# Attention with two-by-two Strassen products: splitting one product of weights and V once more

## The chip, the core and the metric

The kernel runs on one NeuronCore of a Trainium2 chip. The metric is the device time of one execution in microseconds (us). Engines are named as in the profile: PE (TensorE matmul), PEld (its weight loads), DVE (VectorE), ACT (ScalarE), POOL (GpSimd), SP (SyncE, which only issues DMAs here).

## The reference

```python
def setup_inputs():      # q, k, v: (8, 2048, 512) float32, normal
    ...
def reference(q, k, v):
    d_k = q.shape[-1]
    scores = np.matmul(q, k.transpose(0, 2, 1)) / np.sqrt(d_k)
    attn_weights = special.softmax(scores, axis=-1).astype(np.float32)
    return np.matmul(attn_weights, v)
```

## The kernel before

**Tiling.** For each of 8 batches, the 2048 queries are cut into two *spans* of 1024, and a span into two halves of 512 (4 query tiles of 128 in each half). Both matrix products are done in float16 by Strassen's scheme in Winograd's form: 7 products of half-size blocks in place of 8, with sums of blocks before and after.

**Scores (class `Group`).** A group is a pair of neighbouring key blocks (keys 2j and 2j+1, 128 keys each) against both halves of the queries; it has 7 products, each of two 128x512 matmuls (L291). The results collect in PSUM banks x, y, z. After products 1, 5 and 6 ACT copies a bank out (L301, L305, L308), after 7 and 3 DVE adds (L311, L314), after 4 and 2 ACT takes the exponential into `left[1]` and `left[0]` (the unnormalised weights of the first 512 queries), and `exp_right` takes that of 1024 columns into `right` (those of the second 512). Eight groups make a span's weights.

**Weights times V (class `Pair`).** A pair is one query tile of the first half together with one of the second; a span has 4 pairs. `left[0]`, `left[1]` are the weights of a tile of the first half for even and odd key blocks, `right` those of the second half, and V is cut by even and odd key block and by halves of its 512 columns. Each of the 7 products is a sum over 8 key-block pairs j: 8 matmuls with 256 (or 257) columns (L386). The 257th column is a column of ones, which gives the row sums of the softmax. Product 2 is `left[1]` (odd keys) times the first half of V's columns, and belongs to one output quadrant alone. After products 5 and 3 DVE takes the reciprocal of a row sum (L418, L424); ACT scales a bank by it into an output tile (L395), DVE adds the next bank, scaled, to the tile (`final`, L398), and SP stores the tile.

**Rounds and order.** The work runs in 32 rounds g, two for each span. In round g, PE does the pairs a and b of the round, and at the same time the scores of the span after (4 groups, 28 products); each engine executes strictly in the order in which the program issues to it. The order is set by lists: `QORDER` says in which order the products of two neighbouring groups alternate, `ORDER` after which score product a pair's product stands (`b7'` is product 7 of the pair b of the round before), `PLAN` when loads and DMA transposes of the next batch are issued, `KSUMS`, `VSUMS`, `SUMS0` and `sums_of` when DVE makes the sums of K, V, Q and the weights. Round 0 and the last two rounds have lists of their own (`FIRST`, `ALONE`, `LAST`); the opening, before round 0, has word lists (`SECOND`, `OPENING`).

**Buffers.** All eight PSUM banks are in use: qx (2), qy, qz for the scores, px (2), py, pz for the pairs. Output tiles come from a pool of 7, loads of K and Q from a staging pool of 3, and the weights from a pool that holds two spans.

Of the kernel before, what the change touches and what calls it, by code (L numbers as in the profile page):

```python
# [12 lines left out]
def kernel(  # L13
# [21 lines left out]
    nc = tc.nc  # L35
# [29 lines left out]
    ppool = ctx.enter_context(tc.tile_pool(name="ppool", bufs=2))  # L65
    spool = ctx.enter_context(tc.tile_pool(name="spool", bufs=2))
    opool = ctx.enter_context(tc.tile_pool(name="opool", bufs=7))
# [14 lines left out]
    ident = const.tile([P, P], F16)  # L82
    ident_dram = nc.inline_tensor(np.eye(P, dtype=np.float16), name="attn_identity")
    nc.scalar.dma_start(out=ident[:], in_=ident_dram.ap())
# [14 lines left out]
    vt4 = const.tile([P, NJ, H], F16, name="vt4")  # L99
    staged = {}  # L100
# [47 lines left out]
    def transposed(what, c, n, w, copy):  # L148
        src = staged[what, 0, c]
        tr = psum["px"].tile([P, 2, ND, P], F16, tag="px", name="tr")  # L150
        for m in range(w):
            for dc in range(ND):
                nc.tensor.transpose(  # L153
                    tr[:, m, dc, :], src[:, n + m, dc * P:(dc + 1) * P], ident[:]
                )
        copy(out=raw_of(what, 0, c)[:, n:n + w], in_=tr[:, 0:w])  # L156
        if n + w == CH:
            staged.pop((what, 0, c))
# [62 lines left out]
    def new_p(sp):  # L221
        left = [ppool.tile([P, NJ, QH], F16, tag=f"left{s}", name=f"left{s}") for s in range(2)]
        right = ppool.tile([P, NJ, 2, QH], F16, tag="right", name="right")
        pts[sp] = (left, right)
# [124 lines left out]

    class Pair:  # L350
# [3 lines left out]
        def __init__(self, g, which):  # L354
            self.g, self.which, self.done = g, which, 0

# [37 lines left out]
        def scaled(self, out_, src, r):  # L394
            nc.scalar.activation(out=out_, in_=src, func=COPY, scale=r[:])  # L395

        def final(self, out_, src, r):
            nc.vector.scalar_tensor_tensor(  # L398
                out=out_, in0=src, scalar=r[:], in1=out_, op0=MULT, op1=ADD
            )  # L400
# [14 lines left out]
        def after5(self):  # L415
            self.o2 = opool.tile([P, D], F32, tag="o")
            self.r2 = small.tile([P, 1], F32, tag="r2")
            nc.vector.reciprocal(out=self.r2[:], in_=self.z[:, H:H + 1])  # L418
            self.scaled(self.o2[:, H:D], self.z[:, 0:H], self.r2)

        def after3(self):
            self.o1 = opool.tile([P, D], F32, tag="o")
            self.r1 = small.tile([P, 1], F32, tag="r1")
            nc.vector.reciprocal(out=self.r1[:], in_=self.z[:, H:H + 1])  # L424
# [6 lines left out]
        def after6(self):  # L431
            self.scaled(self.o1[:, H:D], self.x[:, 0:H], self.r1)
# [8 lines left out]
        def after4(self):  # L441
            if not self.apart:
# [5 lines left out]
                out=self.o2[:, one], in0=self.x[:, one], scalar1=self.r2[:], scalar2=None, op0=MULT  # L448
# [7 lines left out]
    def pv(g, which):  # L456
        g -= which.endswith("'")
# [7 lines left out]
    ORDER = "a1 b7' a5 b4' a3 b1 a6 a2 a7 b5 a4 b3 b2 b6".split()  # L465
    FIRST = "a1< b1< a1> a5 b1> a3 a2 a6 a7 b5 a4 b3 b2 b6".split()
    ALONE = "b7' a1 b4' a5 b1 a3 b5 a2 a6 b3 a7 b2 b6 a4".split()
    LAST = "b7' a1 b4' a5 b1 b5 a3 a2 b3 a6 b6 a7 b7 b2 b4 a4".split()

# [3 lines left out]
    def after_slot(g):  # L473
        order = {0: FIRST, NP - 2: ALONE, NP - 1: LAST}.get(g, ORDER)
        return {2 * n + 1: x for n, x in enumerate(order)}

    PLAN = {}
    for qt_, slot_, *what_ in (  # L480
# [10 lines left out]
    ):  # L491
        PLAN.setdefault((qt_, slot_), []).append(what_)

    KSUMS = {(1, 14): 0, (2, 0): 1, (2, 16): 2, (3, 2): 3}
    background = deque()

    def prefetch(g, slot):
        b, qt = divmod(g, NQT)
        if (g, slot) == (0, 12):
            nc.gpsimd.memset(vraw[1][:, :, 1, D:D + 1], 1.0)  # L500
        for kind, what, c in PLAN.get((qt, slot), ()):
            if b + 1 < B:
                if kind == "load":
                    load_v(b + 1, c) if what == "v" else load(what, b + 1, c)
                else:
                    dma_transpose(what, b + 1, c)
        if (qt, slot) in KSUMS and b + 1 < B:
            background.extend(k_sums(KSUMS[qt, slot]))
        if background and slot in ((2, 8, 10, 14, 16, 24, 26)):
            background.popleft()()  # L510

    def sums_of(g, slot):

        if g == 0:
            return [first_sum(x) for x in SUMS0.get(slot, "").split()]
        todo = []
        if slot in (7, 9, 11, 13):
            todo.append(p_sums(g, "b")[(slot - 7) // 2])
        early = (20, 23, 25, 27) if g == NP - 2 else (17, 19, 21, 22)
        if slot in early and g + 1 < NP:  # L520
            todo.append(p_sums(g + 1, "a", 0, NJ if g % 2 == 0 else NE)[early.index(slot)])
        if slot in (4, 5) and g % 2 == 0:
            late = p_sums(g, "a", NE)
            todo.extend(late[0:2] if slot == 4 else late[2:4])
        sp = g // 2 + 2
        if slot in (23, 25, 27) and g % 2 == 1 and sp < NP // 2:
            todo.append(q_sums(sp)[(slot - 23) // 2])
        if slot == 6 and g % 2 == 0 and g < NP - 2:
            todo.append(q_sums(sp - 1)[3])
        if g % NQT == 0 and slot in VSUMS:  # L530
            for at in (i for i, s in enumerate(VSUMS) if s == slot):
                todo.append(v_sums(g // NQT, at % NCH)[at // NCH])
        return todo

    SUMS0 = {
        2: "v02",
        3: "v03",
        4: "q3",  # L540
        5: "a0",
        6: "a1",
        8: "a3",
        9: "a2",
        11: "v12 v13",
        12: "v20 v21",
        13: "v22",
        14: "b0 v23",
        15: "v30",
        16: "b1 v31",  # L550
        17: "v32",
        18: "v33",
        19: "b3",
        20: "k02",
        21: "b2",
        22: "A0",
        23: "k12 A1",
        24: "A2",
        25: "k22 A3",
        26: "k32",  # L560
    }

    def first_sum(x):
        n = int(x[1])
        if x[0] in "kv":
            return (k_sums if x[0] == "k" else lambda c: v_sums(0, c))(int(x[2]))[n]
        if x[0] == "q":
            return q_sums(1)[n]
# [205 lines left out]
```

## Time and profile before

| | |
|---|---|
| time, median of 3 runs | 800.87 us (800.75 to 801.21) |
| span of the profiled execution | 799.2 us (its page lists no other time of its own) |
| PE busy | 793.7 us, 99% |
| PEld busy | 538.1 us, 67% |
| DVE busy | 557.6 us, 70% |
| ACT busy | 572.0 us, 72% |
| POOL busy | 71.5 us, 9% |
| granted PE clock | 1.000 |

The span goes from the first instruction to the last in one execution taken by the hardware profiler. Busy time is the share in which the engine has an instruction running; matmuls are pipelined, and one's listed duration (273 ns at 256 columns) is longer than the distance to the next.

### The profile page before, as it was taken

To read this page: it belongs to the slowest core of one execution; us is meant where nothing else is said; L and a number is where in the kernel's file an instruction comes from. 1 tells how busy PE (TensorE), PEld (TensorE's weight loads), DVE (VectorE), ACT (ScalarE), POOL (GpSimd) and SP (SyncE) were. 2 spreads that over 40 slices of the span, in tenths; PEclk is the share of its full clock that TensorE was granted. 3 is DMA by queue.
4 is the path that set the end of the run, shared out by engine and by line. 5 is a ranking of instruction groups with operands and counts; after the bars stand their busy time and mean duration, and the time that the engine had idled before them with its cause. 6 is when DMAs were issued, how large, how long until landed. Compare 5 with 4: busy or idle time off the path is not lost.

```text
span 799.2 us, 14622 instructions
## 1 busy us (share of the span) xinstructions
PE 793.7 (99%) x5556; PEld 538.1 (67%) x5556; DVE 557.6 (70%) x1230; ACT 572.0 (72%) x1020; POOL 71.5 (9%) x105
## 2 busy tenths in 40 slices
PE   9999999999999999999999999999999999999998
PEld 6566666666666666666666666666666666666677
DVE  5786767857677676866768667686776857678564
ACT  4877777777777767777777777777677777776752
POOL 4011110001101010010100110001110011000000
PEclk9999999999999999999999999999999999999999
DMA  9999992899828999399994999849993598711112
GB/s 222 175 176 177 207 172 73 156 183 196 166 60 156 182 197 145 80 161 178 177 158 78 173 177 186 128 93 155 203 217 86 96 205 160 162 40 41 44 52 104
DMA packets 188870, 115.80 MB, mean 145 GB/s; under 512 B 122496, under 2 KB 171904, under 8 KB 188800
## 3 DMA queue, kind: packets, MB, share of 16 engines
q0 software_dynamic: 49648, 49.29, 42.9%
q1 hardware_dynamic: 138576, 65.16, 38.3%
q8 instruction: 43, 0.70, 0.4%
q10 hardware_dynamic: 576, 0.43, 0.2%
q14 instruction: 27, 0.22, 0.1%
HBM read 100.70 MB, written 33.55 MB: 168 GB/s over the span
## 4 chain that ended last, share of the span: by engine, by line
PE 99%; DMA 0%; DVE 0%; ACT 0%; issue 0%
PE t L386 49%; PE t L291 46%; PE t L234 1%; PE t L250 1%; PE tr L153 1%; DMA first<-in_q_dram 0%; PE t L657 0%; DVE kraw L156 0%; ACT o L395 0%; DVE stage L132 0%; DVE o L447 0%
## 5 line engine op out<-in xcount | busy, mean ns | idle before, releaser
L291 PE MATMUL t<-qraw,kraw 128*128 128x512 f16 x732 | 198.1, 379 | 0.0
L395 ACT ACTIVATE o<-t,r 128x256 f32<-128x256 f32 (+1 forms) x256 | 121.1, 473 | 100.5 <-DVE r L418 69.5
L386 PEld LDWEIGHTS <-s 128*128 128x128 f16 x1536 | 150.3, 98 | 56.5
L227 ACT ACTIVATE left<-t 128x512 f16<-128x512 f32 x256 | 154.1, 603 | 37.0 <-PE t L291 30.8
L398 DVE SCALAR_TENSOR_TENSOR o<-t,r,o 128x256 f32<-128x256 f32 x192 | 92.4, 482 | 102.1 <-PE t L386 60.9
L291 PEld LDWEIGHTS <-kraw 128*128 128x128 f16 x984 | 96.2, 98 | 64.2 <-issue 0.3
L291 PE MATMUL t<-qs,ks 128*128 128x512 f16 x492 | 136.5, 379 | 0.0
L386 PE MATMUL t<-vh,left 128*128 128x256 f16 x1024 | 133.0, 273 | 0.0
L386 PE MATMUL t<-vt,s 128*128 128x257 f16 (+1 forms) x1024 | 133.0, 273 | 0.0
L227 ACT ACTIVATE right<-cz 128x1024 f16<-128x1024 f32 x123 | 130.5, 1061 | 1.1 <-DVE cz L311 1.1
L386 PEld LDWEIGHTS <-left 128*128 128x128 f16 x1024 | 100.2, 98 | 37.6
L386 PEld LDWEIGHTS <-right 128*128 128x128 f16 x1024 | 100.2, 98 | 37.5 <-issue 0.4
L305 ACT COPY cz<-t 128x512 f32<-128x512 f32 x122 | 71.4, 585 | 72.8 <-PE t L291 72.4
L311 DVE TENSOR_TENSOR cz<-t,cz 128x512 f32<-128x512 f32 x123 | 84.5, 687 | 52.8 <-PE t L291 52.7
L314 DVE TENSOR_TENSOR cz<-t,cz 128x512 f32<-128x512 f32 x123 | 84.9, 690 | 43.0 <-PE t L291 41.6
L291 PEld LDWEIGHTS <-ks 128*128 128x128 f16 x738 | 72.1, 98 | 48.3 <-DVE ks L183 0.3
L291 PE MATMUL t<-qraw,ks 128*128 128x512 f16 x246 | 73.2, 379 | 0.0
L291 PE MATMUL t<-qs,kraw 128*128 128x512 f16 x246 | 73.2, 379 | 0.0
L301 ACT COPY t<-t 128x512 f32<-128x512 f32 x121 | 69.0, 570 | 4.0 <-PE t L291 0.8
L308 ACT COPY cz<-t 128x512 f32<-128x512 f32 x123 | 71.5, 581 | 0.0
L386 PE MATMUL t<-vh,s 128*128 128x257 f16 x512 | 66.7, 273 | 0.0
L386 PE MATMUL t<-vh,right 128*128 128x256 f16 x512 | 66.2, 273 | 0.1
(62 smaller groups left out, 574.0 us busy)
## 6 DMA issues: line engine op xcount, KB each, us to landing
out_dram<-o SPq DMA_DIRECT2D x124, 256.0 KB, 3.5
vh<-in_v_dram POOLq DMA_DIRECT2D x32, 512.0 KB, 10.5
stage<-in_k_dram POOLq DMA_DIRECT2D x29, 512.0 KB, 8.0
stage<-in_q_dram POOLq DMA_DIRECT2D x28, 512.0 KB, 7.9
right<-in_k_dram POOLq DMA_DIRECT2D x2, 512.0 KB, 13.2
out_dram<-o SPq DMA_DIRECT2D x6, 128.0 KB, 1.7
first<-in_q_dram SPq DMA_DIRECT2D x2, 256.0 KB, 3.3
cz<-in_q_dram SPq DMA_DIRECT2D x2, 256.0 KB, 4.8
```

What stands on the lines that cost most here:

```text
L153: nc.tensor.transpose(tr[:, m, dc, :], src[:, n + m, dc * P:(dc + 1) * P], ident[:])
L227: nc.scalar.activation(out=out_, in_=in_, func=EXP, scale=inv_sqrt_d)
L234: nc.tensor.matmul(st[:], kops[c][0][:, n, dc, :], qraw[0][:, half * NT:(half + 1) * NT, dc, :], start=(dc == 0), stop=(dc == ND - 1),)
L291: nc.tensor.matmul(dst[:], lhs[:, j, dc, :], rhs[:, :, dc, :], start=(n in (1, 5) and dc == 0), stop=(dc == 1), skip_group_check=True,)
L301: self.edges[0](out=self.y[:], in_=self.x[:])
L305: self.edges[1](out=self.cz[:, 1, :], in_=self.z[:])
L308: nc.scalar.copy(out=self.cz[:, 0, :], in_=self.x[:])
L311: nc.vector.tensor_add(self.cz[:, 1, :], self.x[:], self.cz[:, 1, :])
L314: nc.vector.tensor_add(self.cz[:, 0, :], self.z[:], self.cz[:, 0, :])
L386: nc.tensor.matmul(dst[:, 0:width], lhs(j), rhs(j), start=(first and j == 0), stop=(j == NJ - 1), skip_group_check=True,)
L395: nc.scalar.activation(out=out_, in_=src, func=COPY, scale=r[:])
L398: nc.vector.scalar_tensor_tensor(out=out_, in0=src, scalar=r[:], in1=out_, op0=MULT, op1=ADD)
```

## The change

In 15 of the 16 spans (all but the last), product 2 of the four pairs leaves the pairs. What it computed is one matrix product of 512 query rows x 1024 odd keys by 1024 keys x 256 columns of V for the whole span; a new class `Leaf` does it by Strassen's scheme once more. Its blocks are two query tiles by four key blocks against four key blocks by 128 columns. Each of its 7 products is 2 tiles x 4 matmuls with 128 columns, into the bank py, which the pairs of those spans no longer use.

The parts around it:

- `leaf_v_sums` are four sums of the V blocks (128x512 each) once a batch, one of them in place. `leaf_p_sums` are four sums of the weights (128x1024 each) for each span; they are written into the half of `left[0]` that the pairs have finished with.
- A pair's product 1 is now copied by ACT into an accumulator tile `acc` (`after1`), without scaling. After each leaf product, DVE adds its bank into a quarter of an accumulator. After leaf products 3 and 4 an accumulator is complete: POOL multiplies it by the reciprocals, in two instructions, and SP stores it as a half row for two tiles.
- A pair's product 6 now goes to a tile of half rows (`ohpool`) that is stored by itself; products 4 and 7 work as before.
- The leaf of a span runs in L2 and L1 in the span's second round, and in L5, L6, L3, L7, L4 in the first round of the next span.
- The weights lie in fixed tiles in place of a pool; the identity and the zeros of the opening lie in tiles of V's sums; the output pool shrinks from 7 to 3, with 3 accumulators and 2 half-row tiles beside it.
- The lists `ORDER`, `FIRST`, `ALONE`, `LAST`, `PLAN`, `KSUMS`, `VSUMS`, `SUMS0` give way to one word list for each kind of round. A "." is the next score product, "e" an `exp_right`, a, b and L are products of pairs and leaf, s, w, x, y, z, v, k, q are sums (leaf's weights, leaf's V, weights, V, K, Q), l and t are loads and transposes.

```diff
+    def leaf_p(sp):
+
+        a = pts[sp][0][1]
+        w = NT // 2 * P
+        room = pts[sp][0][0]
+        return (a[:, 0:NK, 0:w], a[:, NK:NJ, 0:w], a[:, 0:NK, w:2 * w], a[:, NK:NJ, w:2 * w],
+                room[:, NK:NJ, 0:w], room[:, NK:NJ, w:2 * w])
+
+    def leaf_p_sums(sp):
+        a11, a12, a21, a22, x, y = leaf_p(sp)
+        return {
+            1: lambda: add(x, a21, a22),
+            2: lambda: sub(y, x, a11),
+            3: lambda: sub(x, a11, a21),
+            4: lambda: sub(y, a12, y),
+        }
...
+        def product(self, n):
+            a11, a12, a21, a22, x, y = leaf_p(self.sp)
+            b11, b12, b21, b22, t1, t2, t3, t4 = leaf_v(self.sp // NSP)
+            if n in (1, 2):
+                self.t = bank("py")
+            lhs, rhs, at = {
+                1: (a11, b11, 0), 2: (a12, b21, 0), 3: (y, b22, 1), 4: (a22, t4, 0),
+                5: (x, t1, 1), 6: (y, t2, 0), 7: (x, t3, 0),
+            }[n]
+            for t in range(2):
+                to = self.t[:, (2 * at + t) * P:(2 * at + t + 1) * P]
+                for j in range(NK):
+                    nc.tensor.matmul(
+                        to, lhs[:, j, t * P:(t + 1) * P], rhs[:, j, :],
+                        start=(n in (1, 2) and t == 0 and j == 0), stop=(j == NK - 1),
+                        skip_group_check=True,
+                    )
...
+            nc.vector.tensor_add(acc, part, acc)
+            if n == 3:
+                self.store(0)
+            elif n == 4:
+                self.store(1)
+
+        def store(self, m):
+            acc = acc_of(self.sp, m)
+            for t in range(2):
+                r = r1s[:, self.sp % 2, 2 * m + t:2 * m + t + 1]
+                nc.gpsimd.tensor_scalar(
+                    out=acc[:, t, :], in0=acc[:, t, :], scalar1=r, scalar2=None, op0=MULT
+                )
...
+        def after1(self):
+            if self.leaf:
+                acc = acc_of(self.g // 2, self.i // 2)
+                nc.scalar.copy(out=acc[:, self.i % 2, :], in_=self.x[:, 0:H])
...
         def after6(self):
+            if self.leaf:
+                o = ohpool.tile([P, H], F32, tag="oh", name="oh")
+                self.scaled(o[:], self.x[:, 0:H], self.r1)
+                self.final(o[:], self.z[:, 0:H], self.r1)
...
-    ORDER = "a1 b7' a5 b4' a3 b1 a6 a2 a7 b5 a4 b3 b2 b6".split()
...
+        1: (
+            "w0 lk3 . a1 . . xb0 . b7' . lv1 e . w1 a5 . . xb1 tk1 . w3 e xb3 w2 . b4' . a3 . xb2 lk2 "
+            "a6 . . . b1 . . L2 . . k00 . tk2 e xa0 b5 xa1 a7 k20 . . . xa3 a4 s1 . q0 b3 . e . q1 q2 "
+            "k30 L1 . xa2 s2 b6 . k10 "
+        ),
...
+        0: (
+            "v01 . . L5 lq0 e v03 . a1 b7' ya0 v00 v02 s3 . ya1 L6 ya2 . . ya3 v10 a5 q3 . v11 . s4 "
+            "b4' xb0 lq1 . . e xb1 a3 v12 . L3 v21 v20 . v13 lk0 . tq0 b1 xb2 . xb3 a6 L7 . v22 . v23 "
+            "lv0 . . e v30 xa0 b5 tq1 v32 v33 . a7 xa2 . xa1 L4 . tk0 v31 . xa3 . . b3 lk1 a4 . . e . "
+            ". b6 "
+        ),
...
+        'alone': (
+            "L5 b7' . a1 s3 L6 e s4 ya0 xb0 . ya1 b4' ya3 a5 L3 b1 ya2 L7 xb1 a3 xb3 b5 L4 xb2 a6 b3 "
+            "a7 xa0 a2 b6 b2 xa2 xa1 xa3 a4 "
+        ),
+        'last': (
+            "b7' a1 a5 xb0 xb1 b4' a3 xb2 b1 xb3 b5 a2 b3 q0 a6 b6 a7 q2 b7 a4 b4 b2 q1 "
+        ),
...
```

The lists keyed 1, 2, 3, 0 stand for rounds with that remainder by 4; 0 is the round that opens a batch.

More of the change, by code (lines that the diff above doesn't have):

```diff
@@ L221, in new_p @@
     def new_p(sp):
[L222 to L224 removed]
+        pts[sp] = (lefts[sp % 2], rights[sp % 2])
     def exp(out_, in_):
@@ L350, with leaf @@
+    leaves = {}
+    def leaf(sp, n):
+        if not leaf_span(sp) or sp < 0:
+            return
+        if sp not in leaves:
+            leaves[sp] = Leaf(sp)
+        leaves[sp].product(n)
     class Pair:
@@ L456, in pv @@
     def pv(g, which):
+        if which[0] == "L":
+            leaf(g // 2 - (g % 2 == 0), int(which[1]))
+            return
+        if which[1] == "2" and leaf_span(g // 2):
+            return
         g -= which.endswith("'")
```

280 lines of the change are left out of this document (152 added, 128 removed), and 17 rows, old and new, of tables (PLAN, SEQUENCES).

## The prediction

> **What bounds the kernel now.** I read the page first: the busy times and the chain that ended last.
>
> ```profile
> PE 793.7 (99%) x5556; PEld 538.1 (67%) x5556; DVE 557.6 (70%) x1230; ACT 572.0 (72%) x1020; POOL 71.5 (9%) x105
> ...
> PE 99%; DMA 0%; DVE 0%; ACT 0%; issue 0%
> PE t L386 49%; PE t L291 46%; PE t L234 1%; PE t L250 1%; PE tr L153 1%; DMA first<-in_q_dram 0%; PE t L657 0%; DVE kraw L156 0%; ACT o L395 0%; DVE stage L132 0%; DVE o L447 0%
> ```
>
> PE is the whole chain. A busy PE may still be PE that waits, so I then read what one matmul costs in the chain in order of time, at the opening (the only place with 128-wide matmuls) and in a middle round.
>
> ```profile
> 9.65 0.45 PE t L250 x8
> ...
> 11.21 0.67 PE t L250 x12
> ```
>
> ```profile
> 142.18 0.86 PE t L291 x4
> 143.05 0.88 PE t L386 x8
> 143.93 0.86 PE t L291 x4
> ```
>
> Both first runs are 128 columns wide, with new weights for each matmul: 0.67/12 = 55.9 ns. A 256-wide one takes 109.3 ns (0.874/8), a 512-wide one 215.8 ns. From 46 to 766 us I added up these paces over all matmul starts: idle between them is under 0.2 us. So only fewer PE columns, or a new wait, can move the time.
>
> Then DVE, the next limit, in a round that opens a batch (it holds the 16 V sums), and its queue there.
>
> ```profile
> 138.50:162.90 24.40, 24.40 (x171) 16.50 (x170) 18.43 (x43) 17.78 (x33) 2.84 (x5) 1.00 0.83 149
> ```
>
> ```profile
> 148.08 0.48 DVE L398 SCALAR_TENSOR_TENSOR o<-t,r,o 128x256 f32<-128x256 f32 x1
> 148.47 0.41 DVE L217 TENSOR_TENSOR vh<-vh 128x512 f16<-128x512 f16 x1
> 148.81 0.68 DVE L311 TENSOR_TENSOR cz<-t,cz 128x512 f32<-128x512 f32 x1
> 149.41 0.42 DVE L217 TENSOR_TENSOR vh<-vh 128x512 f16<-128x512 f16 x1
> ```
>
> DVE (fourth column) is 18.43 of 24.40 us busy. The queue shows that an instruction starts 0.08 us before its predecessor's listed end (148.08 + 0.48 against 148.47). So DVE's real price is the listed duration less 0.083; for ACT the same comparison gives 0.105 less.
>
> **The change, part by part.**
>
> *PE.* Removed: product 2 of four pairs in 15 spans, 15 x 4 x 8 = 480 matmuls of 256 columns, 480 x 109.3 ns = 52.4 us. Added: 7 leaf products x 2 query tiles x 4 key blocks = 56 matmuls of 128 columns per span, 840 x 55.9 ns = 47.0 us. Net -5.5 us. Weight loads rise by 360, but each hides behind the matmul before it already at 55.9 ns pace. In the rounds' L250 rows nothing separates 12 such matmuls in a row, and a leaf product is 8.
>
> The page "TensorE: Matmul & The Clock Gate" of the Trainium skill (section "Back-to-back issue gap") gives 81 ns per matmul for a sustained stream of 128-wide load-and-multiply pairs, and 55.6 ns without the loads. The trace disagrees with the first and agrees with the second: 55.9 ns, loads included. By 81 ns the leaf would cost 68.0 us, and the sum would be +15.6 us.
>
> *DVE per span.* Removed: 4 finals of after2, 4 x (0.482 - 0.083) = 1.6 us. Added: 7 adds of 128x256 f32 out of PSUM. No row has this form. The 128x512 add (L311, 0.687) less 256 elements at 0.96 per ns gives 0.42; the 256-wide final (L398) is 0.482, the upper end; I take 0.42, for it is the same operation. 7 x 0.34 = 2.4. Four leaf sums of 1024 f16 elements like L340, 4 x 0.60 = 2.4; two halves of the four leaf sums of V, 2 x 0.33 x 2 = 0.7 (half a batch). Net +3.9 us per span of 48 us. DVE isn't the bound by sum: the batch-opening round goes from 18.4 to about 20.5 of 24.8 us.
>
> *ACT.* One copy after product 1 in place of one scaling after product 3, at the same 128x256 (0.47): nothing, except that it no longer waits for the reciprocal.
>
> *The order.* DVE's room decides by place, not by sum, so I laid the words of a batch on a sheet: PE at 0.4315 for ".", 0.874 for a pair's product, 0.447 for a leaf's; DVE and ACT in their order at the prices above, each instruction 0.2 us behind its last matmul's end of streaming. The old order laid out this way has no PE word late in any round, which is what the trace shows. In the new order no word is late by more than 0.03 us. The tightest place is in the batch-opening round (seven of them: rounds 4, 8, ... 28), the 26th ".": product 4 of a group, which needs DVE's add of product 7. PE reaches it at 25 x 0.4315 + 11 x 0.874 + 5 x 0.447 = 22.64 us. DVE gets the final of b7' at 3.69 us and from there has no idle time before that add: 3 finals 1.20, 4 short sums 0.81, 14 V sums 4.66, 2 leaf sums 1.19, 4 leaf adds 1.35, 5 cz adds 3.03, 3 reciprocals 0.24, the query sum 0.60, 8 weight sums 4.78: 17.86 us, so 21.55; the add 0.69 and 0.07 to PE: 22.31. Spare: 0.33 us. With leaf adds at 0.48 it is 0.1 us. I book 0.1 us for all such places.
>
> *POOL and SP.* Four multiplies of 128x256 f32 per span on POOL. The trace has no such row: below it lies the 128x1 copy (0.183), above it DVE's 256-wide final (0.482); I take 0.33. Behind them on POOL stand loads whose tiles are wanted a round later, behind the two leaf stores on SP the transposes: k's chunk 0 is issued near 19 us of a batch-opening round, lands in 7.2 us and is summed some 13 us into the next round, so 2 us of waiting is covered; beyond about 10 us it would not be. Stores go from 8 to 10 per span, in the same bytes. Buffers: the half-row tiles (2) are reused a round later, 24 us against 3.5 us to landing. Each of these: nothing.
>
> *Opening and end.* The opening's words are the same; its buffers move into tiles that are not in use yet: nothing. Round 30 has the last leaf without removed work (counted above, since all 15 leaves are). Its pair b waits for an accumulator tile that the first leaf store frees: 5.3 us of PE from L3 to b3 against 0.6 + 0.7 + 3.5 + issue, about 5; bound 0 to 0.5. After the last matmul now a 256-wide final and a 128 KB store (0.48 + 1.7) stand where a 128-wide scaling and a 64 KB store stood (0.37 + 1.6): +0.2.
>
> *Sum.* -5.5 + 0.1 + 0.1 + 0.2 = -5.1 us. The span of 799.2 becomes 794.1; 1.7 us lie outside the span (the median of the runs shown is 800.87), so 795.8. By nearest rows the ends are 795.0 (no end cost, the 0.4 us of waits in the old last rounds gone too) and 797 (leaf adds at 0.55: 0.2 us late in each batch-opening round).
>
> **The rivals.**
>
> *POOL's multiplies hold DVE up* (slower). If a multiply that reads the accumulator keeps DVE's sums from starting, each of the four in a batch-opening round adds its length h to the queue above: 4h - 0.33 us late, seven times, and h - 0.07 late in the round before, seven times (an exp two groups back there has no room). Together 7 x (5h - 0.4): zero at h = 0.08, the whole gain of 5.1 at h = 0.23. At 0.183 it costs 3.6 (799.4), at 0.33 8.8 (804.6), at 0.48 14 (809.8). For it: DVE has no idle time there. Against it: POOL starts only when DVE's instruction lets it, adds and finals that read PSUM stand in between, and the DVE sums that ran beside POOL's DMA issues kept 0.416 and 0.68 us; but those issues read no tile. If half of the multiplies hold, it ends near 800.
>
> The page "SBUF — State Buffer" of the Trainium skill (section "Who interferes with whom") says that a VectorE instruction with two SBUF inputs contends with a GpSimd instruction that reads SBUF, and the second one to start blocks fully. That is this rival; no run here shows it yet.
>
> *The 128-wide matmuls run slower in the leaf than at the opening* (slower). The gain is gone at 52.4/840 = 62.4 ns. The only measured pace, 55.9, is 11% below: a chance of 0.03.
>
> *The order stalls elsewhere*: the exps of the span after next write the left weights in which the leaf still reads, and ACT is strictly in order. A stall of 0.35 us in each of 15 spans takes the gain. On the sheet these exps come several us after the last leaf sum: a chance of 0.09.
>
> *The change buys nothing*: PE columns are saved but the order gives them back. The chain leaves no place for that but new waits, which are the cases above.
>
> **How the numbers follow.** The forecast of 795.8 (795.0 to 797.2): 0.58. POOL's hold: 0.30, split by how many multiplies hold: 0.12 below 799.3, 0.06 between, 0.12 above 802.5. Slower leaf matmuls 0.03, slower. Other stalls 0.09: 0.01 faster, 0.01 none, 0.07 slower. A difference of 0.2% (1.6 us) is about what a measurement of this kernel can tell from no change; so faster 0.71, same 0.07, slower 0.22. Below 795.0 I leave 0.05, above 802.5 about 0.14; the range is 795.0 to 802.5, and the likeliest case's own is 795.0 to 797.2.
>
> **What would show it.** Right: 840 matmuls of 128 columns on a new line at 0.45 us per eight in the chain, PE 99% of it, a span near 794, DVE near 620 us busy, no row "PE waits for DVE or ACT" over 1 us in total in the middle. Wrong: DVE sums listed longer than 0.42 or 0.69 us beside POOL's multiplies, PE idle in the batch-opening rounds before L291 (POOL's hold); runs of eight leaf matmuls over 0.5 us; ACT exps that wait for DVE sums.

## The result: 6.4% slower

The changed kernel takes 852.64 us, median of six executions (845.84 to 870.26), against 800.92 us (800.54 to 801.21) for the kernel before on the same chip: a ratio of 1.0637, 95% interval 1.0600 to 1.0673. The forecast was 795.8 with a range to 802.5. The profile below is of the slowest of the six executions (870.26 us, span 868.5), which the ratio leaves out; the others left no profile, but their mean granted clock (0.974 to 0.980, against 0.969 here and 1.000 before) is low as well.

The page of the changed kernel, busy times and the chain that ended last:

```profile
PE 806.2 (93%) x5916; PEld 543.0 (63%) x5916; DVE 617.9 (71%) x1367; ACT 576.2 (66%) x1020; POOL 146.0 (17%) x165
...
PEclk9999999979799999999999989999799998999999
...
PE 74%; DMA 22%; DVE 2%; issue 1%; ACT 1%; POOL 0%; ACTq 0%; DVEq 0%; SPq 0%; POOLq 0%
PE t L299 35%; PE t L495 33%; DMA kraw<-stage 17%; PE t L421 5%; DMA out_dram<-acc 3%; DMA right<-in_k_dram 1%; PE t L242 1%; DVE cz L322 1%; DMA first<-in_k_dram 0%; DVE s L348 0%; DVE o L507 0%; PE tr L163 0%; POOL right L128 0%; ACT o L504 0%; ACT cz L316 0%
```

Before, PE was 99% of the chain and DMA 0%. Now 17% of the chain is one kind of transfer, `kraw<-stage`: the DMA transposes of the next batch's keys. The matmuls themselves did get cheaper: at the paces of the prediction, all matmuls together take 784.2 us against 789.7 before, the forecast 5.5 us. But between 46 and 766 us the starts of PE's matmuls now lie 75 us further apart than these paces allow, where it was less than 0.2. The account closes: 75 - 5.5 = 69.5, and the span grew by 69.3 us.

Not all of the 75 us is standing. The run e12 below has the same 5916 matmuls and no stall; against its page PE is not busy for 57 us more here, and it is busy for 18 us more (806.2 against 788.2). These 18 us are matmuls at half pace: at the stalls the granted clock is 0.50 for 3.4 to 10.2 us (seven such stretches, the first from 179.84 to 190.08 us), and just after the first stall eight 256-wide matmuls take 1.87 us ("184.53 1.87" below) in place of 0.88. Where this text says that PE loses some us, it means both together.

Four rounds of one batch of the changed kernel, from its first score product to that of the next round (columns: length, then busy time of PE, PEld, DVE, ACT and POOL, granted clock, DMA share, GB/s):

```profile
134.31:159.15 24.84, 24.84 (x195) 17.12 (x193) 22.25 (x54) 17.47 (x32) 7.29 (x6) 1.00 0.45 81
159.15:192.47 33.32, 26.36 (x171) 16.82 (x169) 17.15 (x37) 18.32 (x34) 3.76 (x5) 0.85 1.19 174
192.47:218.17 25.70, 25.70 (x202) 17.85 (x201) 20.41 (x46) 18.37 (x34) 7.22 (x8) 1.00 1.25 127
218.17:252.96 34.79, 24.56 (x163) 15.62 (x161) 17.07 (x36) 17.94 (x33) 0.74 (x1) 0.85 0.78 109
```

The batch-opening round takes 24.84 us, just what the forecast's sheet gave for it, though DVE has least room there. The stalls of this batch are in the second and fourth rounds (23.49 and 22.61 us where nothing stalls), and the stretches at half clock bring the mean clock of these rounds to 0.85; the PEclk row shows the same dips. Over the whole execution the second round stalls in five of seven batches (32.3 to 35.1 us) and the third in one (33.0); the fourth is longer in the first three only.

The chain in order of time, the SP queue and the POOL queue of the changed kernel around the first of these stalls, and what DVE waited for in the whole span:

```profile
163.65 0.56 PE t L495 x6
164.21 17.76 DMA kraw<-stage
181.99 0.04 DVE ks L191
...
184.53 1.87 PE t L495 x8
...
190.45 0.45 PE t L421 x8
...
216.83 15.14 DMA out_dram<-acc
```

```profile
149.59 0.38 SPq L444 DMA_DIRECT2D out_dram<-acc  x1
150.08 7.80 SPq L153 DMA_TRANSPOSE qraw<-stage  x1
...
164.21 6.44 SPq L153 DMA_TRANSPOSE kraw<-stage  x1
...
172.21 11.98 SPq L153 DMA_TRANSPOSE kraw<-stage  x1
```

```profile
146.14 3.42 POOL L439 TENSOR_SCALAR acc<-acc,r1s 128x256 f32<-128x256 f32 x2 [35.22 <-DVE acc L429]
149.51 0.79 POOL L128 DMA_DIRECT2D stage<-in_k_dram  x1
150.30 0.75 POOL L217 DMA_DIRECT2D vh<-in_v_dram  x1
155.17 2.38 POOL L439 TENSOR_SCALAR acc<-acc,r1s 128x256 f32<-128x256 f32 x2 [4.12 <-ACT t L309]
163.92 0.79 POOL L128 DMA_DIRECT2D stage<-in_k_dram  x1 [6.36 <-DMA qraw<-stage]
166.01 0.74 POOL L128 DMA_DIRECT2D stage<-in_k_dram  x1 [1.31 <-DMA qraw<-stage]
166.75 0.75 POOL L217 DMA_DIRECT2D vh<-in_v_dram  x1
```

```profile
DVE ks L191 <- DMA kraw<-stage: 56.2, 9, 9.9
```

Read together: the transpose of key chunk 0 (`tk0`) is issued at 164.21; three loads (0.5 MB each, POOL's queue) are issued from 163.92 on; the last packet of the transpose is moved 17.2 us after its issue. DVE, strictly in order, stands at the first sum of K (L191), behind which stands the add that frees PE's bank. In the whole span DVE stands there nine times, 56.2 us. The other kind, `out_dram<-acc`, is a store that SP issued at 216.77, behind a transpose of Q whose issue had held it for 14.2 us, and that landed 15 us later still, so that an accumulator came free late. In the whole span ACT waits for stores (of accumulators and output tiles) five times, 30.8 us.

For comparison, the same transposes in the profile before, queue of SP:

```profile
143.63 2.55 SPq L143 DMA_TRANSPOSE qraw<-stage  x1
...
156.29 1.85 SPq L143 DMA_TRANSPOSE kraw<-stage  x1
```

They issue 7.2 and 8.7 us earlier in the round (which starts at 135.07 us there and at 134.31 here), hold SP for a third of the time, and land 4.4 and 4.0 us after issue. (The landing of a single transpose is counted here, and below, to its last packet; the medians to landing that are quoted from the page's list are counted to its semaphore, which comes 0.5 us later or more.)

**Why a transpose beside loads is slow** can be counted in the packets of the trace. A transpose is 2048 packets of 256 bytes on the hardware queue, a load 512 packets of 1024 bytes on the software queue, both over the same 16 DMA engines. Beside nothing a transpose's packet takes 18 ns, and the transpose runs 2.6 us. A load's packet takes 96 ns. Where loads were pending for the whole of a transpose, 2011 to 2126 load packets were moved while it ran (13 such transposes in four kernels' profiles): one for one. Each engine then moves 128 packets of either kind, 128 x (18 + 96) ns = 14.6 us (16.3 with the 31 ns that a transpose's packet takes beside loads); these transposes ran 13.8 to 15.2 us. By this estimate the price is some 6 us per MB of loads beside it, and at most about 12 us per transpose. It is a low estimate where loads come and go: `tk0` above ran 14.9 us with 1.5 MB beside it, 8 us per MB over the 2.6. With under 0.05 MB beside it a transpose of the changed kernel takes 2.2 us (median), and 21 of the 56 after the opening had over 0.7 MB beside them, against 4 of 56 before.

The Trainium skill states the rule behind this count (page "DMA: Bandwidth & Descriptors", section "Queues, rings and completion order"): each DMA engine takes turns between the queue rows that have work for it, one packet at a time. The trace agrees, with one load packet for each transpose packet in the profile's counting.

### The profile page after: what moved, and what is told of

It is laid out like the page before. It is cut to its first block, busy times and chain, and to the rows that moved or that the text cites. A ratio compares the mean times of both kernels' runs of the same rounds, so it can differ in the third digit from the quotient of the medians.

```text
span 868.5 us, 15651 instructions
## 1 busy us (share of the span) xinstructions
PE 806.2 (93%) x5916; PEld 543.0 (63%) x5916; DVE 617.9 (71%) x1367; ACT 576.2 (66%) x1020; POOL 146.0 (17%) x165
## 4 chain that ended last, share of the span: by engine, by line
PE 74%; DMA 22%; DVE 2%; issue 1%; ACT 1%; POOL 0%; ACTq 0%; DVEq 0%; SPq 0%; POOLq 0%
PE t L299 35%; PE t L495 33%; DMA kraw<-stage 17%; PE t L421 5%; DMA out_dram<-acc 3%; DMA right<-in_k_dram 1%; PE t L242 1%; DVE cz L322 1%; DMA first<-in_k_dram 0%; DVE s L348 0%; DVE o L507 0%; PE tr L163 0%; POOL right L128 0%; ACT o L504 0%; ACT cz L316 0%
## 5 line engine op out<-in xcount | busy, mean ns | idle before, releaser
L299 PE MATMUL t<-qraw,kraw 128*128 128x512 f16 x732 | 195.2, 380 | 12.8 <-ACT left L235 12.8
L495 PEld LDWEIGHTS <-s 128*128 128x128 f16 x1536 | 152.8, 100 | 64.0 <-issue 5.0
L299 PE MATMUL t<-qs,ks 128*128 128x512 f16 x492 | 146.3, 390 | 2.0 <-DVE cz L322 1.9
L235 ACT ACTIVATE right<-cz 128x1024 f16<-128x1024 f32 x123 | 130.2, 1059 | 20.5 <-DVE cz L319 18.3
L439 POOL TENSOR_SCALAR acc<-acc,r1s 128x256 f32<-128x256 f32 x60 | 73.8, 1233 | 375.9 <-ACT right L235 217.3
L504 ACT ACTIVATE o<-t,r 128x256 f32<-128x256 f32 (+1 forms) x128 | 60.4, 475 | 110.9 <-DVE r L532 64.5
L495 PE MATMUL t<-vt,right 128*128 128x256 f16 x512 | 70.3, 284 | 37.4 <-DVE o L507 37.4
L495 PE MATMUL t<-vh,s 128*128 128x257 f16 x512 | 72.5, 288 | 1.2 <-ACT o L504 1.2
L495 PE MATMUL t<-vh,left 128*128 128x256 f16 x544 | 70.8, 273 | 0.0
L421 PEld LDWEIGHTS <-left 128*128 128x128 f16 x840 | 55.8, 98 | 21.5 <-issue 1.0
## 6 DMA issues: line engine op xcount, KB each, us to landing
vh<-in_v_dram POOLq DMA_DIRECT2D x32, 512.0 KB, 11.7
```

Source lines behind the costliest of these rows:

```text
L235: nc.scalar.activation(out=out_, in_=in_, func=EXP, scale=inv_sqrt_d)
L299: nc.tensor.matmul(dst[:], lhs[:, j, dc, :], rhs[:, :, dc, :], start=(n in (1, 5) and dc == 0), stop=(dc == 1), skip_group_check=True,)
L421: nc.tensor.matmul(to, lhs[:, j, t * P:(t + 1) * P], rhs[:, j, :], start=(n in (1, 2) and t == 0 and j == 0), stop=(j == NK - 1), skip_gro ...
L439: nc.gpsimd.tensor_scalar(out=acc[:, t, :], in0=acc[:, t, :], scalar1=r, scalar2=None, op0=MULT)
L495: nc.tensor.matmul(dst[:, 0:width], lhs(j), rhs(j), start=(first and j == 0), stop=(j == NJ - 1), skip_group_check=True,)
L504: nc.scalar.activation(out=out_, in_=src, func=COPY, scale=r)
```

## The experiments

Theory: loads of the next batch now run while its transposes run, because the new order and the queues of POOL and SP bring the two together; the stretched transposes come too late for DVE's sums. Rivals: the places of the words alone; the multiplies on POOL alone (through DVE, or through the queue); the accumulators' buffers.

**e1_dma_back: ten words put back.** The loads and transposes of the first two rounds of a batch go back to their times of the kernel before; the rest stays.

```diff
 0: (
-    "b4' xb0 lq1 . . e xb1 a3 v12 . L3 v21 v20 . v13 lk0 . tq0 b1 xb2 . xb3 a6 L7 . v22 . v23 "
+    "b4' xb0 lq1 tq0 . . e xb1 a3 v12 lk0 . L3 v21 v20 . v13 . b1 xb2 . xb3 a6 L7 . v22 tq1 . "
...
 1: (
-    "w0 lk3 . a1 . . xb0 . b7' . lv1 e . w1 a5 . . xb1 tk1 . w3 e xb3 w2 . b4' . a3 . xb2 lk2 "
+    "w0 . a1 . . xb0 . b7' . e . w1 a5 . . xb1 . w3 e xb3 w2 . b4' tk1 lk2 . a3 . xb2 a6 . . "
...
```

> The changed kernel with the ten load and transpose words of the first two rounds of a batch (lk0, tq0, tq1, tk0, lk1; tk1, lk2, lv1, tk2, lk3) put back at the times in the round that they had before the change; nothing else moves. Theory A (the places of the transfers: the first Q transpose is issued 4 us later than before, and lk3 and lv1 19 and 8 us earlier, so the K transposes run beside loads and land after DVE has come to the sum k00; DVE, in order, stands there, and PE behind it): the waits of DVE for kraw's transposes (56 us in the profile after) go below 5 us and the time falls to 796 to 803 us. Theory B (POOL's multiplies, 0.9 to 1.8 us each, delay the loads behind them on POOL and, through the leaf stores, the transposes behind them on SP): the multiplies stay, so the time stays above 840 us.

Measured: 798.29 us (795.11 to 806.83, ten executions), ratio 0.9981 (0.9951 to 1.0012). In the profiled execution (795.11) every round takes 24.84, 23.49, 25.70 or 22.61 us and PE never stands between 46 and 766 us: its span of 793.3 is 0.8 from the forecast's 794.1. So 54 us of the 57 between forecast and result hang on ten words that start transfers and compute nothing. The leaf, the multiplies and the buffers are those of the changed kernel, so none of them has to cost anything by itself. The scatter to 806.83 may mean that transfers still meet in some executions; none of those was profiled.

**e2_round0, e3_round1, e6_lk0_only, e7_tq0_only: parts of e1.** Only the words of list 0, only those of list 1, and of list 0 only `lk0` or only `tq0`, each as in e1's diff (e6 and e7):

```diff
-    "... v12 . L3 v21 v20 . v13 lk0 . tq0 b1 ..."
+    "... v12 lk0 . L3 v21 v20 . v13 . tq0 b1 ..."      (e6)
+    "b4' xb0 lq1 tq0 . . e xb1 a3 v12 . L3 ... lk0 . b1 ..."      (e7)
```

> The changed kernel with only the five words of the batch-opening round put back (lk0, tq0, tq1, tk0, lk1), the second round's as changed. Theory A, if the late transposes of Q start it: most of the stall goes, 797 to 810 us; if the early loads lk3 and lv1 are what slows the K transposes: 830 to 855 us. Theory B: above 840 us.

> The changed kernel with only the five words of the second round put back (tk1, lk2, lv1, tk2, lk3); the batch-opening round as changed. Theory C (a load that runs beside a transpose stretches it, some 8 us per MB, and everything that brings the two together counts: the multiplies on POOL, lv0 behind the leaf's L7, lk3 and lv1 early): tq0 still shares the DMA engines with lk0 and lv0, but 1.0 MB less runs beside tk0 and tk1, so the time lies between, 805 to 835 us. If the batch-opening round alone decides: 840 to 865.

> The changed kernel with one word moved: lk0 stands before L3, so on POOL's queue the load of K's chunk 0 is ahead of the leaf store's two multiplies and can be issued as soon as its buffer is free. Theory A1 (the first transpose of Q is late: on SP it stands behind the leaf store, which waits for the multiplies): tq0 is issued near 150 us as before, the stall stays, 835 to 865 us. Theory A2 (tq0 and lk0 are released together by the multiplies and share the DMA engines): lk0 is gone by then, tq0 lands in 6 to 8 us instead of 13.8, and the time falls to 797 to 815 us.

> The changed kernel with one word moved: tq0 stands at 7.4 us of the batch-opening round as before the change, so ahead of the leaf store of L3 on SP. Theory A1: tq0 is issued near 142 us and lands in 5 to 6 us, the rest follows earlier, 797 to 815 us. Theory A2: the same, since lk0 still waits for the multiplies and so comes after tq0; only a time above 830 us would speak against both, and for the early loads lk3 and lv1 of the next round.

Measured, one execution each: 805.43, 841.13, 841.40 and 818.42 us. PE loses 9.4, 45, 46.4 and 22.9 us in the middle. e2 lies in its range and e6 comes out as its theory A1 says; e3 and e7 miss theirs (805 to 835 and 797 to 815) by 6 and 3 us. The places of list 0 matter most. `tq0` back alone lands in 3.9 us and takes two thirds of the loss away, but the transposes behind it still meet loads (tq1 11.8, tk0 12.1, tk1 16.7 us to landing); `lk0` alone does little, since `tq0` is what stands behind the leaf's store on SP.

**e4_no_mult: no multiplies on POOL**, in the changed order (their part of the output stays unscaled).

```diff
-            for t in range(2):
-                r = r1s[:, self.sp % 2, 2 * m + t:2 * m + t + 1]
-                nc.gpsimd.tensor_scalar(
-                    out=acc[:, t, :], in0=acc[:, t, :], scalar1=r, scalar2=None, op0=MULT
-                )
```

> The changed kernel without the two multiplies on POOL before each leaf store (the first half of the columns of the first-half queries is stored without its division by the row sums; that part of the output is left unscaled). Theory A: POOL's 74 us of multiplies were not in the way; the time stays at 840 to 870 us, with DVE's waits for kraw's transposes over 40 us. Theory B: loads and leaf stores no longer wait for POOL; the time falls to 796 to 810 us.

Measured: 800.75 us, one execution, PE losing 5.2 us. The transposes still take 11.2 and 11.3 us to landing (medians), but POOL runs ahead, and they are issued earlier (`tk0` at 155.72 us, 8.5 before the changed kernel's). So the multiplies decide the loss in this order: not by their own time on an engine (73.8 us in a span of 868.5, and nobody reads their result but a store), but by what stands behind them. Words and multiplies cause it together: e1 keeps the multiplies and moves ten words, e4 keeps the words and drops the multiplies, and each undoes the loss.

**e5_before_late and e5b_before_late: the kernel before, with the new places.** The entries of `PLAN` are put where the changed order has them; no leaf, no multiplies.

```diff
-        (0, 8, "trans", "q", 0), (0, 16, "trans", "q", 1),
...
+        (0, 12, "load", "k", 0), (0, 12, "trans", "q", 0), (0, 16, "load", "v", 0),
+        (0, 18, "trans", "q", 1), (0, 21, "trans", "k", 0),
...
-        (1, 8, "load", "k", 2), (1, 20, "trans", "k", 2),
+        (1, 11, "load", "k", 2), (1, 17, "trans", "k", 2),      (e5; e5b has 1, 19)
...
```

> The kernel before the change, with no leaf in it, whose plan of loads and transposes gets the places (to the nearest slot) that the changed kernel gives them. Theory A: it stalls in the second round of each batch as the changed kernel does, at 820 to 860 us. Theory B: there is no multiply on POOL, so it stays at 799 to 804 us.

> The kernel before with the changed kernel's places of loads and transposes, the transpose tk2 two slots later than in e5, so that it follows the last product that reads the old chunk. It has neither leaf stores on SP nor multiplies on POOL. Theory A with the places alone to blame: 815 to 860 us. If it takes the multiplies or stores in the queues as well (loads then run ahead on POOL here): 800 to 810 us.

e5 gave 861.12 us, but says nothing on the theory: its `tk2` stood ahead of the last product that reads the old chunk, and PE waited for that in each batch. e5b, two places later, gave 800.61, one execution: no loss. The places alone are harmless in the kernel before: a load waits for the transpose that frees its staging buffer, POOL reaches each one early, and in the batch of the rounds shown above the transposes land in 4.4 to 7.2 us, with 0.04 MB or less beside them. That was a miss for the rival of the places, and it sent me to the queue of POOL.

**e11_before_mult: e5b with four more multiplies per span on POOL**, of the leaf's form, into a scratch tile that nothing reads.

```diff
+        def twice(self, src, r):
+            if self.g % 2 == 0 and 2 <= self.g < NP - 2:
+                for t in range(2):
+                    nc.gpsimd.tensor_scalar(
+                        out=scratch[:, t, :], in0=src, scalar1=r[:], scalar2=None, op0=MULT
+                    )
```

> The kernel before with the changed kernel's places of loads and transposes (as e5b) and four extra POOL multiplies of 128x256 f32 in the first round of each span, two after product 3 of pair a and two after product 5 of pair b, into a scratch tile that nothing reads. Theory B (multiplies in POOL's queue are enough): 815 us or more. Theory C: they pin lk0 and lk1 to their places, but the V loads still run ahead early, so the damage is partial: 800 to 815 us.

Measured: 816.0 us, one execution, on the border of the two ranges; PE loses 14.8 us, and DVE stands at the K sums (L182) for 17.0. No matmul, sum or accumulator of the change is in this kernel; its pool of output tiles is one smaller, to make room for the scratch tile, and DVE once waits 3.4 us for a multiply that still reads an output tile. Multiplies that stand in POOL's in-order queue ahead of loads are thus enough to lose most of 15 us, where the places alone lost nothing. The rest of the changed kernel's 52 us is not reproduced here; this kernel has no leaf stores on SP.

**e8_spread, e9_v_late, e10_both: moving transfers to the quieter rounds.** e8 is e1 with `lq2`, `lq3`, `lv2` at the end of the third round and `tq2`, `tq3`, `lv3` in the fourth. e9 is the changed kernel with only the V loads moved, behind L4 of the third round and into the fourth. e10 takes both.

```diff
 2: (
-    "lv3 k22 L4 . . b3 xa1 a4 . . . b6 xa3 k12 . . . e . xa2 "
+    "L4 . . b3 xa1 a4 . . lv0 . b6 xa3 k12 lv1 . . . e . xa2 "      (e9)
...
 3: (
-    "b7' k32 k03 . . . e a1 . a5 b4' . xb0 xb2 . . . . a3 . k13 xb1 . xb3 . e k23 . . b1 . . "
+    "b7' k32 k03 . . . e a1 lv2 . a5 b4' . xb0 xb2 . . . . a3 . k13 xb1 lv3 . xb3 . e k23 . . "      (e9)
+    "b7' k32 k03 . . tq2 . e a1 . a5 b4' . xb0 xb2 . . tq3 . . a3 . k13 xb1 lv3 . xb3 . e k23 "      (e8)
```

> The changed kernel with the places of e1, and the transfers that are not wanted before the next batch moved out of the round that K's transposes need: lq2, lq3 and lv2 go to the end of the third round, tq2, tq3 and lv3 to the fourth, in which DMA is at 0.24 in the kernel before. Theory A: K's transposes land faster than in e1 (9.0 us median), so the executions with a late one go away: median 795 to 796 us and all runs within 2 us. If another cause made e1's runs spread from 795 to 807, they spread here as well, with a median of 797 to 799.

> The changed kernel with its four V loads in the third and fourth round of a batch in place of the first three (V is wanted only in the next batch); multiplies and all else as changed. Theory C: 1.0 MB less beside the transposes of the first two rounds, time 800 to 825 us. If the multiplies on POOL are the cause by themselves (theory B): above 835 us.

> The changed kernel with the K and Q transposes of e8 and with all four V loads in the third and fourth round. Theory C: the transposes of the first two rounds run nearly alone and land in 4 to 8 us; PE idle in the middle under 0.5 us, median 794.8 to 796 us, all runs within 3 us. If the spread of e1 and e8 has another cause, it stays: 794 to 800.

Measured: e8 797.17 us (794.64 to 799.43), ratio 0.9943 (0.9927 to 0.9960); e9 807.58, one execution, PE losing 12.6 us; e10 842.15 us (838.63 to 843.70), ratio 1.0502 (1.0480 to 1.0524). e9 lies in the range of theory C. e8 missed its 795 to 796 us, and its runs spread over 4.8 us, not 2. e10 was meant to be the best, and missed by over 40 us. Its POOL queue, and what DVE waited for:

```profile
207.87 1.82 POOL L439 TENSOR_SCALAR acc<-acc,r1s 128x256 f32<-128x256 f32 x2 [5.45 <-ACT o L504]
209.63 1.53 POOL L128 DMA_DIRECT2D stage<-in_q_dram  x2
211.15 2.98 POOL L217 DMA_DIRECT2D vh<-in_v_dram  x4
214.09 0.79 POOL L128 DMA_DIRECT2D stage<-in_q_dram  x1
```

```profile
DVE qs L208 <- DMA qraw<-stage: 45.4, 7, 8.4
```

Seven loads leave in a row once POOL is done with L4's multiplies, `lv2` and `lv3` of places later in the order among them, and the transposes `tq2` and `tq3` that I had moved there meet 2.1 MB: a run of 15.05 us, one packet for one. The stall moved from the K sums to the Q sums, and from the second rounds to the next batch-opening ones. A miss of place, and a repeat of the mechanism.

**e12_apart: K and Q as in e1, V loads as in e9**, and `tq2`, `tq3` left where they are, so that no V load is beside a transpose.

```diff
 0: (
-    "lv0 . . e v30 xa0 b5 tq1 v32 v33 . a7 xa2 . xa1 L4 . tk0 v31 . xa3 . . b3 lk1 a4 . . e . "
+    "v23 . . e v30 xa0 b5 v32 v33 . a7 xa2 tk0 . xa1 L4 . v31 . xa3 lk1 . . b3 a4 . . e . . "
...
 2: (
+    "L4 . . b3 xa1 a4 . . lv0 . b6 xa3 k12 lv1 . . . e . xa2 "
```

**e13b_beside: e12 with the V loads put beside transposes on purpose** (the four words leave lists 2 and 3 for these places); **e14_apart_no_mult: e12 without the multiplies** (unscaled as in e4).

```diff
 0: (
-    "v23 . . e v30 xa0 b5 v32 v33 . a7 xa2 tk0 . xa1 L4 . v31 . xa3 lk1 . . b3 a4 . . e . . "
+    "v23 . . e v30 xa0 b5 v32 v33 . a7 xa2 lv0 tk0 . xa1 L4 . v31 . xa3 lk1 . . b3 a4 . . e . "      (e13b)
...
 1: (
-    "w0 . a1 . . xb0 . b7' . e . w1 a5 . . xb1 . w3 e xb3 w2 . b4' tk1 lk2 . a3 . xb2 a6 . . "
+    "w0 . a1 . . xb0 . b7' . e . w1 a5 . . xb1 . w3 e xb3 w2 . lv1 lv2 lv3 b4' tk1 lk2 . a3 . "      (e13b)
```

> All that the changed kernel computes, with the ten words for K and Q of the first two rounds at the times of the kernel before (as in e1) and the four V loads of the next batch moved behind L4 of the third round and into the fourth, so that no V load is in flight when a transpose of the first two rounds starts. Theory (a transpose that meets loads in flight is stretched by about 6 to 8 us for each MB beside it, VectorE stands at its sum and TensorE behind it): the transposes of the first two rounds run alone, 2.4 to 3.3 us each, PE idles under 2 us in the middle, rounds are 24.84, 23.49, 25.70 and 22.61, and the time is 794.5 to 796.5 us in nearly every execution, so its spread is under 3 us where e1 had 11.7. Rival (the multiplies on POOL cost by themselves, through the leaf store that SP waits for): single executions still reach 800 us and more, as in e1, and the kernel without the multiplies is ahead by over 2 us.

> The kernel of e12_apart with the V loads put beside transposes on purpose: one (0.5 MB) in list 0 just ahead of tk0, three (1.5 MB) in list 1 just ahead of tk1; no place of a leaf, a multiply, a store or a transpose is altered. Theory: tk0 runs 5 to 8 us in place of 2.6, tk1 11 to 16 us, tk1 is late by some 5 to 9 us in each of seven batches and the rounds with it, and the time is 815 to 860 us. Rival (the transposes are late only since SP and POOL issue them late, and the transport is wide enough for both): the time of e12 within 2 us, transposes still at 2.4 to 3.3 us.

> The kernel of e12_apart without POOL's two multiplies of each leaf (that part of the output stays unscaled). Theory: where loads and transposes are apart nothing that matters stands behind the multiplies, so the time is that of e12 within 1 us (794 to 796.5). Rival (the multiplies cost by themselves): ahead of e12 by over 2 us, towards 791 to 793.

**e12** took 795.44 us, median of five (794.59 to 795.87), against 800.90 (800.46 to 801.96): ratio 0.9928 (0.9916 to 0.9940). It has the lowest median of all kernels here, beats both the kernel before and the changed one, and lies 0.4 us from the forecast. From its page (span 793.8 us), and the rounds of one batch:

```profile
PE 788.2 (99%) x5916; PEld 537.2 (68%) x5916; DVE 618.6 (78%) x1367; ACT 576.6 (73%) x1020; POOL 146.6 (18%) x166
```

```profile
132.54:157.38 24.84, 24.84 (x194) 17.10 (x192) 22.25 (x54) 17.47 (x32) 7.30 (x6) 1.00 0.51 113
157.38:180.87 23.49, 23.49 (x171) 15.78 (x169) 16.92 (x36) 18.29 (x34) 1.48 (x2) 1.00 1.03 176
180.87:206.57 25.70, 25.70 (x202) 17.91 (x201) 20.59 (x47) 18.36 (x34) 9.71 (x12) 1.00 0.78 142
206.57:229.18 22.61, 22.61 (x162) 15.00 (x160) 17.05 (x36) 18.07 (x33) 0.42 (x1) 1.00 1.03 187
```

PE is busy for the whole of each round and the clock is 1.00. The work on every engine is that of the changed kernel; one transpose of 56 after the opening has over 0.7 MB beside it. The same bytes are moved and one V load more (33 in place of 32; DMA share 1.03 in two rounds), only at other times.

**e13b** took 800.89 us, one execution. The first half of its expectation holds for `tk1`, which runs 10.4 to 12.2 us in five of the six batches after the first; `tk0` meets loads in one of them alone and runs 2.1 to 3.8 us in the others, not 5 to 8. The key transposes together take 14.6 us to landing (median, the page's list of transfers), against 6.1 in e12.

```profile
168.20 8.30 SPq L153 DMA_TRANSPOSE kraw<-stage  x1
...
185.69 9.67 SPq L153 DMA_TRANSPOSE kraw<-stage  x1
```

The second half is a miss: PE loses 6.0 us in all, and the time is 5 us above e12's, not 20 to 65. In this order `tk1`, the first of the two lines, lands 15.7 us after its issue, and its first sum is at 184.67: 16.5 us of room, just enough. In the changed kernel `tk0` was issued at 164.21, and its first sum, as far into the round as in e12 (14.5 us), was due at 173.7: 9.5 us of room for a transpose that took 17.2. So loads beside transposes are not enough for the loss of the changed kernel; the transposes must be late as well. Four kernels make a square of it (transposes early or late, V loads away from them or beside them): e12, early and away, 795.4; e13b, early and beside, 800.9; e9, late and away, 807.6, where K loads still meet them; the changed kernel, late and beside, 852.6. (e13b and e9 are one execution each; e1's ten lie up to 11.7 us apart, so the middle two are rough.)

**e14** was expected within 1 us of e12 by the theory, and over 2 us ahead of it by the rival. It took 806.40 us (799.14 to 814.57, twelve executions), ratio to the kernel before 1.0056 (1.0032 to 1.0080): 11 us slower with less work. Both were wrong. POOL's queue in e14, and in e12:

```profile
179.00 2.97 POOL L217 DMA_DIRECT2D vh<-in_v_dram  x4
```

```profile
199.97 1.83 POOL L439 TENSOR_SCALAR acc<-acc,r1s 128x256 f32<-128x256 f32 x2 [5.46 <-DVE acc L429]
201.74 3.02 POOL L217 DMA_DIRECT2D vh<-in_v_dram  x4
```

In e12 POOL comes to its V loads straight from L4's multiplies. Without them the four V loads leave 23 us earlier, and `tk3` takes 15.2 us to landing; what stands behind it is pushed on, Q loads and `tq3` meet, and that takes 15.4. What PE then loses in e14's profile (7.6 us) is not at the sums: DVE waits for no transpose of K or Q there. PE waits twice, for 2.3 and 3.6 us, for a half-row tile that ACT may not write before its store has landed, and the first of the two stores stood on SP behind `tq3`. The chain in order of time has it:

```profile
304.15 14.59 DMA out_dram<-oh
```

In e12 the multiplies are the gate that keeps the loads away; in the changed order the same multiplies hold loads until the transposes come. What a wait on POOL is worth depends on what it pushes into what.

## Why the prediction was wrong

*PE, -5.5 us: right.* 784.2 against 789.7 us by paces; eight leaf matmuls take 0.45 us in the chain ("190.45 0.45 PE t L421 x8"). The rival of slower leaf matmuls did not come: 55.9 ns holds in all 840, and the 81 ns that the Trainium skill gives for such a stream (the page named in the prediction) are not seen. (The +15.6 us that the prediction gives for 81 ns is the PE term alone; with the other terms the sum would be +16.0.)

*DVE: right.* The leaf add estimated at 0.42 us is 0.420 (105 of them), the busy time near 620 is 617.9. The round that opens a batch rose by 2.2 us (20.02 to 22.25, from its first score product to that of the next round; 2.1 forecast) and did not stall. Its level was read 1.6 us too low: the prediction's window, 138.50 to 162.90 us, begins 3.4 us into the round, whence 18.4 and 20.5.

*The rival "POOL's multiplies hold DVE up" (0.30): wrong mechanism.* The lines of the changed kernel for the multiplies and for one of V's sums, which has both inputs in SBUF and runs beside a multiply in 21 of its 32 cases:

```profile
L439 POOL TENSOR_SCALAR acc<-acc,r1s x60: 914/925/1819, 96.5 to 846.5; 128x256 f32<-128x256 f32 x60
```

```profile
L227 DVE TENSOR_TENSOR vh<-vh x32: 412/416/420, 46.8 to 803.0; 128x512 f16<-128x512 f16 x32
```

(Columns: shortest, median and longest in ns.) These sums hold their time to 8 ns; the multiplies take up to twice their shortest. Of all of DVE's sums in the middle two alone, each beside a multiply that had begun first, took clearly longer, by 0.16 us (0.58 us at 324.23, 0.84 at 842.88). POOL is nearly always the one that waits, so no multiply was added to DVE's queue. The Trainium skill has it that the second of the two to start blocks ("SBUF — State Buffer", section "Who interferes with whom"); here it is POOL that waits, but for these two, and the prediction priced DVE's waiting.

*The multiply's size: mis-sized.* Booked at 0.33 us, bounded by 0.18 and 0.48; it is 1.23 on average. A store's two multiplies hold POOL for 1.8 to 3.4 us, not 0.7.

*"POOL and SP ... Each of these: nothing": the step that failed.* It names the place (k's chunk 0, summed some 13 us into the next round) and even a bound ("beyond about 10 us it would not be"), and then takes 7.2 us, a median of the kernel before, as the time to landing. The step counted waits in queues and left out that the two queues that it moves share one transport. In the changed kernel this transpose takes 17.8 us by the measure of that median ("164.21 17.76"), after an issue that itself comes 8.7 us later in the round than before. The rows for it were there before: the two DMA queues of the kernel before have 42.9% and 38.3% of the 16 engines' time, and in its middle two key or query transposes ran 11.9 and 11.6 us beside 0.9 MB of loads, against 2.7 alone. They were issued early enough, so neither DVE nor PE waited and no row of their waits showed them. The same step put the stores at nothing too; stores that stood behind transposes on SP cost the changed kernel 3% of its chain, and e14 its half-row tiles.

*Opening and end: small, as booked, but not in the parts.* After the middle PE stands 0.35 us, against 0.40 before. From the start of the last matmul to the end of the span e12 takes 3.5 us against 3.9 before, where 0.2 us more was forecast; its opening loses 0.4 us more. That e12's span of 793.8 lies 0.3 us from the forecast's 794.1 is in part luck: these two nearly cancel.

What stays open: why some executions of e1 and e8 reach 799 to 807 us. e12, where the V loads are away from the transposes, stays within 1.3 us in five executions, which fits, but there is no profile of a late execution of e1.

## What to carry to other kernels

When an order is rewritten, transfers that compute nothing need the same sheet as the engines: for each transpose its issue, its due time, and the bytes that other queues move meanwhile, at one packet for one packet. A queue that runs in order is also a clock: an instruction put into it, or taken out of it, moves every load behind it, so ask of each load what holds it now and what will hold it then. A duration taken as a median over a kernel is good only for the neighbours that it had there.

## What the runs showed of the hardware

- A DMA transpose of 0.5 MB runs 2.6 us alone and up to 15 us beside loads, because its 256-byte packets (18 ns) take turns with 1024-byte packets (96 ns) one for one. Its issue holds SP's queue meanwhile: 1.8 to 6.1 us in the batch of the kernel before that is compared above, up to 14.2 in the changed kernel, and stores behind it are late too.
- A multiply of 128x256 f32 by a column takes POOL 0.914 us alone and up to 1.82 beside DVE's sums, which keep their time in all but two cases.
- A stall cost more than the standing in the changed kernel: seven times the granted clock was 0.50 for 3.4 to 10.2 us at a stall, and PE was busy 18 us longer for the same matmuls. The 512-wide ones are listed at up to 634 ns there in place of 379.
